# Hybrid decoder block on one core: layer-norm steps with costs of their own, the first head's loads inside the last projection, and a fixed order at the start

## The chip, the cores and the metric

The kernel runs on one core of one Trainium2 chip. The core has five engines that run side by side and are tied together by semaphores: PE (TensorE, matrix products), DVE (VectorE), ACT (ScalarE, function tables), POOL (GpSimd) and SP (SyncE, which here issues the loads and stores). The time is device time in microseconds for one execution; lower is better. The time before is 1504.86 us, the median of two runs (1503.34 and 1506.37).

## The reference, cut to what matters

```python
h = rmsnorm(x, norm_gain)                               # x is 1024 x 1024
proj = h @ w_in                                         # 1024 x 11264
a_val, a_glu, a_gate, q, k, v, r_gate, g_a, g_b = split(proj)
u = a_val * sigmoid(a_glu)
u = depthwise_causal_conv(u, 31 taps) + bias            # each channel alone
u = silu(layernorm(u, ln_g, ln_b))                      # over the 1024 channels
u = u * silu(a_gate)
y_a = u @ w_conv_proj
q, k = rotary(q), rotary(k)                             # 4 heads of 256
o = retention(q, k, v)                                  # causal, chunks of 128 tokens
y_b = (groupnorm(o) * gn_g * silu(r_gate)) @ w_ret_proj
m = sigmoid(g_a) * y_a + sigmoid(g_b) * y_b
out = rmsnorm(x + m @ w_out, final_gain)
```

All of it is float32. Products are formed from a rounded high part and a low remainder of each operand, three matmuls for one.

## The kernel before, in words

**Start.** `row_stats(hf)` squares the half `hf` of x on ACT, adds the squares on DVE (lines 490 to 493), sums them over channels on PE, takes the root on POOL (line 137) and spreads the row factors with a diagonal matrix `dg` (line 503) through PE. `normed` (line 511) multiplies x by them on DVE, `h_split` makes high and low parts. The projections of the first two pairs run beside this.

**Projections.** 88 column blocks of `w_in` are worked off in 44 *pairs* (class `Pair`). A pair forms two blocks for all tokens in seven products (a Strassen scheme) of 12 matmuls of 128x512 each. `prep` builds the seven weight operands on ACT and DVE, in six steps; `use.c` disposes of the results: `Plain` stores them (with Silu for the gates `rg` and `ag`, with Sigmoid for `ga` and `gb`), `Rope` rotates q and k on DVE and POOL and stores them, `Conv` multiplies by the Sigmoid of the gate and queues 31 taps of the convolution. The order is v0, v1, cv0, v2, k0, v3, cv1, q0 and so on (in this document pairs are counted from 0; k pairs are 4, 9, 15 and 20, q pairs 7, 12, 17 and 23, the last conv pair cv7 is 30); the last eight pairs are the gates `ga` and `gb`, all Sigmoid.

**The planner.** The pair loop keeps a budget `left`: after each product it gains `SLOT * FILL` (2.64 us) minus what the product itself costs DVE, then runs at most one `prep` step, and then as many entries of the queue `taps` as the budget holds, each at the price `TAP`. Behind the last conv pair the steps of `layer_norm()` are put behind the taps in the same queue, at the same price each, with empty `idle` steps between. What is left when the pairs are done is emitted behind them.

**Layer norm.** `mean` over `acc`, the sum of the convolution's results; for each of 8 blocks `center`: load `co_d`, subtract `mu` (line 385), store `cd_d`, square on ACT, add; then `var` (16 small matmuls and a root), `rows` (`bcast_rows`: `dg` and two matmuls), and for each block `apply`: load `cd_d` and `ag_d`, multiply by the row factors on DVE (line 411), Silu on ACT (line 412), multiply by `ag` on DVE (line 413), store `u_d` (line 414).

**Heads and output.** Eight half heads follow (class `Head`: `load` of k, q and vT, `keys`, `values`, `main`), with the projections `conv_proj` (which needs all of `u_d` through `load_u`), `ret_proj` and `out_proj` between them. `Weights` loads and splits their weights ahead.

**What sets the order.** Each instruction is written once in the program; a scheduler then places the instructions of each engine, by its own estimate of when they can start, so the order on an engine need not be the order of the code. Each engine works through its own list strictly in order. All loads are issued from SP, in one queue with the stores.

Of the kernel before, what the change touches and what calls it, by code (L numbers as in the profile page):

```python
# [11 lines left out]
ALU = mybir.AluOpType  # L12
# [3 lines left out]
NK = D // P  # L16
# [3 lines left out]
TAPS = 31  # L20
# [9 lines left out]
N_SMALL = 8 * TAPS + 8 * 4 + 16 + H + 4  # L30
W_LIVE = 6
SPLIT_AHEAD = 4
SLOT, TAP, FILL = 2.72, 1.28, 0.97


class Group:
# [7 lines left out]
def hybrid_block_kernel(  # L44
# [70 lines left out]
    def mm(ps, l, r, start, stop, onto=False):  # L115
        nc.tensor.matmul(ps, lhsT=l, rhs=r, start=start, stop=stop, skip_group_check=onto)  # L116
# [22 lines left out]


    taps = deque()

    def flush(n):
        while taps and n > 0:
            taps.popleft()()
            n -= 1

# [165 lines left out]
    class Conv:  # L315
# [8 lines left out]
        def c(self, d, hf, x):  # L324
            cb = self.cb
            if d == 0:
                self.g[hf] = small_t("sg")
                nc.scalar.activation(self.g[hf], x, AF.Sigmoid)
                if hf == 0:
                    self.u = sb.tile([P, 1088], F32, tag="u", bufs=2, name=nm("u"))  # L330
                    nc.gpsimd.memset(self.u[:, :HALO], 0.0)
                return
            u = self.u
            nc.vector.tensor_tensor(u[:, HALO + hf * T:HALO + (hf + 1) * T], x, self.g[hf], ALU.mult)
            if hf == 1:
                return
            box = []

            def first():
                box.append(U("cv"))  # L340
                nc.vector.tensor_scalar(box[0], u[:, 0:S], cw[:, cb, 0:1], cb_[:, cb:cb + 1], ALU.mult, ALU.add)

            def tap(k):
                def go():
                    o = box[0]
                    nc.vector.scalar_tensor_tensor(o, u[:, k:k + S], cw[:, cb, k:k + 1], o, ALU.mult, ALU.add)  # L346
                    if k == TAPS - 1:
                        nc.sync.dma_start(co_d[cb], o)
                        if cb == 0:
                            ln["acc"] = U("acc")  # L350
                            nc.scalar.copy(ln["acc"], o)
                        else:
                            nc.vector.tensor_tensor(ln["acc"], ln["acc"], o, ALU.add)
                        box.clear()
                return go

            taps.append(first)
            taps.extend(tap(k) for k in range(1, TAPS))

    def layer_norm():  # L360

# [52 lines left out]
                nc.sync.dma_start(u_d[cb // 2][cb % 2], d)  # L414
            return go

        def idle():
            pass

        steps += [load(0, co_d), idle, mean, load(1, co_d), idle]  # L420
        for cb in range(NK):
            if cb + 2 < NK:
                steps.append(load(cb + 2, co_d))
            steps.append(center(cb))
        steps += [idle, load(0, cd_d), var, idle, load(1, cd_d), idle, rows, idle]
        for cb in range(NK):
            if cb + 2 < NK:
                steps.append(load(cb + 2, cd_d))
            steps.append(apply(cb))
        return steps  # L430

    def silu(name, n, dst):
# [50 lines left out]
    def row_stats(hf):  # L483
# [16 lines left out]
        r4 = rsqrt(ps[:, :NC], NORM_EPS, NC)  # L500
        dg = small_t("dg", (P, NC, P))
        for c in range(NC):
            nc.vector.tensor_scalar(dg[:, c, :], ident, r4[:, c:c + 1], None, ALU.mult)
        r_row[hf] = bank()
        mm(r_row[hf], ones, dg.rearrange("p c i -> p (c i)"), True, True)

    def normed(hf, js):
        for j in js:
# [23 lines left out]
        next(run0)  # L532
        next(run1)

    row_stats(0)
    prep0[0][0]()
    normed(0, (0, 1))
    h_split("B11", b11)
    row_stats(1)
    prep1[0][0]()  # L540
    normed(0, (2, 3))
    h_split("B21", b21)
    prep0[1][0]()
    prep1[1][0]()
    both()
    normed(1, (0, 1))
    sums(b11, b12, b11)
# [30 lines left out]
        nc.sync.dma_start(cs[i], a["cs"][i])  # L578
    nc.sync.dma_start(dmask, a["dmask"])
    pairs[3].load()  # L580

    left = 0.0
    steps = deque(prep[4:])
    for i in range(2, len(pairs)):
        p = pairs[i]
        nxt = pairs[i + 1] if i + 1 < len(pairs) else None
        for n, cost in enumerate(p.run()):
            if nxt and n == 0:
                nxt.load_xy()
            if n == 3 and i + 2 < len(pairs):  # L590
                pairs[i + 2].load()
            if nxt and n == 2:
                steps.extend(nxt.prep())
            left = min(left + SLOT * FILL - cost, 4.0)
            if steps:
                f, cost = steps.popleft()
                f()
                left -= cost
            while left >= TAP and taps:
                taps.popleft()()  # L600
                left -= TAP
        if isinstance(p.use, Conv) and p.use.cb == NK - 1:
            taps.extend(layer_norm())
        if p is qs[-1]:
            cs = None
    while taps:
        taps.popleft()()


    class Weights:  # L610
        def __init__(self):
# [328 lines left out]
    def free(f):  # L940
        add(lambda w: f(), cost=0)
# [12 lines left out]
        plan[H + 2, c] = ret[1][1][2 * c:2 * c + 2] + conv[1][c:c + 1]  # L954
        plan[H + 3, c] = ret[1][2][2 * c:2 * c + 2] + conv[1][NC + c:NC + c + 1]

    free(heads[0].load)
    free(lambda: halves[0].load_u(None))
    free(heads[0].keys)
    free(lambda: heads[0].values(0))  # L960
    free(lambda: heads[0].values(2))
    late = None
    for i, hd in enumerate(heads):
        nxt = heads[i + 1] if i + 1 < len(heads) else None
# [24 lines left out]
    for n, g in enumerate(groups):  # L989
# [2 lines left out]
            ws.split()  # L992
        while g.cost and ws.n_split < len(ws.seq) and ws.live < g.limit and ws.n_split < need + SPLIT_AHEAD:
            ws.split()
        while g.cost and ws.n_load < len(ws.seq) and ws.n_load < ws.n_split + 2:
            ws.load()
        mine = [ws.ready.popleft() for _ in g.weights]
        g.emit(mine)
# [69 lines left out]
```

## Time and profile before

| what | value |
|---|---|
| median of two runs | 1504.86 us |
| profiled execution, whole time | 1509.48 us |
| its span in the trace | 1507.6 us |
| mean granted clock of PE | 0.977 of full speed |
| PE busy | 1386.6 us, 92% of the span |
| DVE busy | 1158.2 us, 77% |
| ACT busy | 576.7 us, 38% |
| POOL busy | 90.2 us, 6% |
| moved by DMA | 200.80 MB, mean 133 GB/s |

The profiled execution is its span and 1.9 us around it; as a whole it lies 4.6 us above the median of the two timed runs. Busy time is the share of the span in which an engine executes; the profile also cuts the span into 40 slices with the busy tenths of each engine, and there PE shows 9 in nearly all slices, with a dip in the first two and in slices 24 and 25, at about 900 to 945 us.

### The profile page before, as it was taken

What the parts mean: (1) busy time and instruction counts of PE and PEld (TensorE: products, weight loads), DVE (VectorE), ACT (ScalarE), POOL (GpSimd) and SP (SyncE); (2) the same over time, 40 slices, a digit from 0 to 9 for tenths busy, and PEclk for the clock granted to TensorE, in tenths of its full rate; (3) what the DMA queues carried; (4) which work ended last, traced back from release to release, by engine and by line L of the source; (5) the groups of instructions that cost most, each with busy time, mean ns of one, the idle gap of its engine ahead of it and who ended that gap; (6) DMA issues with size and microseconds to landing.
All of it is one profiled execution on the core that took longest, in us unless ns stands there. A gap on an engine that the chain in (4) does not pass through costs nothing.

```text
span 1507.6 us, 16563 instructions
## 1 busy us (share of the span) xinstructions
PE 1386.6 (92%) x6184; PEld 1131.8 (75%) x6184; DVE 1158.2 (77%) x1344; ACT 576.7 (38%) x817; POOL 90.2 (6%) x91
## 2 busy tenths in 40 slices
PE   3899999999999999999999990799999899999998
PEld 2688787887887788888888870687877677777776
DVE  4979989989879979898989465665677757547673
ACT  3453332332233344443443343544544334424321
POOL 1001011011201100000000000000000000000000
PEclk9999999999999999999999995899999999999999
DMA  5143332322323332323333488643443456334331
GB/s 194 58 135 107 107 112 71 112 98 86 125 70 112 106 118 84 126 84 126 112 126 112 164 306 332 241 156 126 140 154 113 130 191 210 121 107 149 123 128 56
DMA packets 95504, 200.80 MB, mean 133 GB/s; under 512 B 8896, under 2 KB 25536, under 8 KB 95424
## 3 DMA queue, kind: packets, MB, share of 16 engines
q1 hardware_dynamic: 94272, 197.65, 38.5%
q10 hardware_dynamic: 1152, 2.10, 0.4%
q8 instruction: 48, 0.79, 0.2%
q14 instruction: 32, 0.26, 0.1%
HBM read 143.09 MB, written 56.62 MB: 132 GB/s over the span
## 4 chain that ended last, share of the span: by engine, by line
PE 66%; DVE 19%; DMA 7%; issue 4%; ACT 3%; POOL 1%; SPq 1%; DVEq 0%; POOLq 0%; ACTq 0%
PE ps L116 64%; DVE cv L346 5%; DVE wl L191 2%; DMA q<-q_d 1%; DMA gb<-gb_d 1%; DVE w L633 1%; DMA d<-co_d 1%; DMA Y<-w_v 1%; DVE G L208 1%; DMA u<-u_d 1%; PE ps L709 1%; DVE h L477 1%; POOL rr L137 1%; DVE ps L254 1%; DVE x L511 1%
## 5 line engine op out<-in xcount | busy, mean ns | idle before, releaser
L116 PE MATMUL ps<-h,wh 128*128 128x512 f32 x2112 | 654.6, 391 | 12.4 <-DVE ps L254 8.6
L116 PEld LDWEIGHTS ps<-h,wh 128*128 128x128 f32 x2112 | 396.1, 188 | 101.9 <-DVE ps L254 11.9
L116 PE MATMUL ps<-h,wl 128*128 128x512 f32 x1056 | 411.4, 390 | 0.3 <-DVE wl L191 0.3
L346 DVE SCALAR_TENSOR_TENSOR cv<-u,small,cv 128x1024 f32<-128x1024 f32 x240 | 311.7, 1299 | 3.5
L116 PEld LDWEIGHTS ps<-h,wl 128*128 128x128 f32 x1056 | 198.4, 188 | 41.9 <-DVE wl L191 0.6
L116 PE MATMUL ps<-oT,w 128*128 128x512 f32 x768 | 192.7, 399 | 6.8 <-DVE yb L838 2.2
L116 PEld LDWEIGHTS ps<-oT,w 128*128 128x128 f32 x768 | 142.4, 189 | 39.2 <-ACT oT L799 3.5
L116 PE MATMUL ps<-h,ws 128*128 128x512 f32 x528 | 127.0, 389 | 2.4 <-DVE x L511 2.4
L116 PEld LDWEIGHTS ps<-h,ws 128*128 128x128 f32 x528 | 99.0, 188 | 23.4 <-DVE x L511 2.9
L116 PE MATMUL ps<-w,m 128*128 128x512 f32 x384 | 94.7, 406 | 8.6 <-ACT w L629 6.3
L116 PEld LDWEIGHTS ps<-w,m 128*128 128x128 f32 x384 | 74.6, 196 | 26.4 <-ACT w L629 7.0
L116 PE MATMUL ps<-u,w 128*128 128x512 f32 x384 | 90.9, 392 | 1.6 <-DVE ga L873 1.1
L116 PEld LDWEIGHTS ps<-u,w 128*128 128x128 f32 x384 | 71.3, 188 | 17.8 <-DVE ga L873 1.9
L190 ACT CAST wh<-G 128x1024 fp32r<-128x1024 f32 (+1 forms) x45 | 46.4, 1034 | 77.3 <-DVE G L208 38.9
L137 POOL TENSOR_TENSOR rr<-rs,neg_half 128x1 f32<-128x1 f32 (+2 forms) x35 | 26.5, 757 | 723.3 <-DVE rs L134 723.3
L208 DVE TENSOR_TENSOR G<-X,N 128x1024 f32<-128x1024 f32 x44 | 55.4, 1259 | 18.0 <-PE ps L116 18.0
L190 ACT CAST wh<-Y 128x1024 fp32r<-128x1024 f32 (+1 forms) x45 | 46.4, 1031 | 58.1 <-DVE Y L217 23.7
L191 DVE TENSOR_TENSOR wl<-Y,wh 128x1024 fp32r<-128x1024 f32 (+1 forms) x45 | 57.6, 1282 | 13.5 <-ACT wh L190 13.3
L285 ACT ACTIVATE o<-ps 128x512 f32<-128x512 f32 x60 | 35.8, 597 | 81.4 <-PE ps L116 75.5
L191 DVE TENSOR_TENSOR wl<-N,wh 128x1024 fp32r<-128x1024 f32 (+1 forms) x45 | 58.2, 1294 | 3.1 <-ACT wh L190 2.0
L191 DVE TENSOR_TENSOR wl<-G,wh 128x1024 fp32r<-128x1024 f32 (+1 forms) x45 | 53.8, 1197 | 6.6 <-PE ps L116 6.0
L200 DVE TENSOR_TENSOR X<-X,Y 128x512 f32<-128x512 f32 x44 | 32.4, 737 | 32.1 <-DMA Y<-w_v 11.2
(122 smaller groups left out, 1562.7 us busy)
## 6 DMA issues: line engine op xcount, KB each, us to landing
raw<-w_ret SPq DMA_DIRECT2D x32, 512.0 KB, 4.7
rg_d<-o SPq DMA_DIRECT2D x32, 256.0 KB, 2.5
raw<-w_conv SPq DMA_DIRECT2D x16, 512.0 KB, 4.4
vT<-v_d SPq DMA_DIRECT2D x16, 512.0 KB, 7.4
rg<-rg_d SPq DMA_DIRECT2D x64, 128.0 KB, 3.0
raw<-w_out SPq DMA_DIRECT2D x16, 512.0 KB, 4.5
v_d<-o SPq DMA_DIRECT2D x24, 256.0 KB, 2.2
x<-xT SPq DMA_DIRECT2D x8, 512.0 KB, 6.4
```

Source lines behind the costliest of these rows:

```text
L116: nc.tensor.matmul(ps, lhsT=l, rhs=r, start=start, stop=stop, skip_group_check=onto)
L137: nc.gpsimd.tensor_tensor(r, s, neg_half[:, :n], ALU.pow)
L190: nc.scalar.copy(hi[:, i], x[:, i])
L191: eng.tensor_tensor(lo[:, i], x[:, i], hi[:, i].bitcast(F32), ALU.subtract)
L200: nc.vector.tensor_tensor(X[:, :T], X[:, T:], Y[:, :T], ALU.add)
L208: nc.vector.tensor_tensor(self.G.rearrange("p (n t) -> p n t", t=T), self.X.rearrange("p (n t) -> p n t", t=T), N[:, :T].unsqueeze(1).broa ...
L254: nc.vector.tensor_tensor(pd, pa, s5, ALU.add)
L285: nc.scalar.activation(o, x, self.func)
L346: nc.vector.scalar_tensor_tensor(o, u[:, k:k + S], cw[:, cb, k:k + 1], o, ALU.mult, ALU.add)
L477: nc.vector.tensor_tensor(lo, x, hi.bitcast(F32), ALU.subtract)
L511: nc.vector.scalar_tensor_tensor(x, x, n_g[:, 2 * j + k:2 * j + k + 1], r_row[hf], ALU.mult, ALU.mult)
L633: nc.vector.scalar_tensor_tensor(lo, t, g, hi.bitcast(F32), ALU.mult, ALU.subtract)
```

## The change

The convolution's taps and the layer-norm steps get a price each in the queue (a load and the mean 0, `center` and `apply` 2.5, `var` 0.2, `rows` 1.8, the last tap of a block `2 * TAP`), and the `idle` steps go; `FILL` goes from 0.97 to 1.04, so a product now gains 2.83 us of budget. With `tc.issue_after(row_stats(0))` the instructions of the block that follows are placed behind the last `dg` of the first half. The pair loop stands behind the classes of the heads, so that the loads of the first head (k, q and the two vT) can be emitted after the fifth product's result of the last pair; `load_u` is emitted behind `keys` and `values`, not between `load` and `keys`. The weights of the later projections are loaded four ahead of their split, not two.

```diff
-SLOT, TAP, FILL = 2.72, 1.28, 0.97
+SLOT, TAP, FILL = 2.72, 1.28, 1.04
...
-            taps.append(first)
-            taps.extend(tap(k) for k in range(1, TAPS))
+            taps.append((first, TAP))
+            taps.extend((tap(k), TAP if k < TAPS - 1 else 2 * TAP) for k in range(1, TAPS))
...
-        def idle():
-            pass
-
-        steps += [load(0, co_d), idle, mean, load(1, co_d), idle]
+        def step(f, cost=0.0):
+            steps.append((f, cost))
+
+        step(load(0, co_d))
+        step(load(1, co_d))
+        step(mean)
         for cb in range(NK):
             if cb + 2 < NK:
-                steps.append(load(cb + 2, co_d))
-            steps.append(center(cb))
-        steps += [idle, load(0, cd_d), var, idle, load(1, cd_d), idle, rows, idle]
+                step(load(cb + 2, co_d))
+            step(center(cb), 2.5)
+        step(load(0, cd_d))
+        step(load(1, cd_d))
+        step(var, 0.2)
+        step(rows, 1.8)
         for cb in range(NK):
             if cb + 2 < NK:
-                steps.append(load(cb + 2, cd_d))
-            steps.append(apply(cb))
+                step(load(cb + 2, cd_d))
+            step(apply(cb), 2.5)
...
-            nc.vector.tensor_scalar(dg[:, c, :], ident, r4[:, c:c + 1], None, ALU.mult)
+            last = nc.vector.tensor_scalar(dg[:, c, :], ident, r4[:, c:c + 1], None, ALU.mult)
         r_row[hf] = bank()
         mm(r_row[hf], ones, dg.rearrange("p c i -> p (c i)"), True, True)
+        return last.ins
...
-    row_stats(0)
-    prep0[0][0]()
-    normed(0, (0, 1))
...
+    with tc.issue_after(row_stats(0)):
+        prep0[0][0]()
+        normed(0, (0, 1))
...
-            while left >= TAP and taps:
-                taps.popleft()()
-                left -= TAP
...
+            while taps and left >= taps[0][1]:
+                f, cost = taps.popleft()
+                f()
+                left -= cost
+            for f in ahead.get((len(pairs) - i, n), []):
+                f()
...
-    free(heads[0].load)
-    free(lambda: halves[0].load_u(None))
-    free(heads[0].keys)
-    free(lambda: heads[0].values(0))
-    free(lambda: heads[0].values(2))
+    ahead = {(1, 4): [heads[0].load]}
...
+    heads[0].keys()
+    while taps:
+        taps.popleft()[0]()
+    heads[0].values(0)
+    heads[0].values(2)
+    halves[0].load_u(None)
...
-        while g.cost and ws.n_load < len(ws.seq) and ws.n_load < ws.n_split + 2:
+        while g.cost and ws.n_load < len(ws.seq) and ws.n_load < ws.n_split + 4:
```

How the instructions stand is shown at four places. The names are the tiles of the program, with a number each; an entry reads result, then operands.

PE at the end of the projections, before. `wh` and `wl` with `h` are the last product of the last pair, `invd, acc` is `var`, `dg, ones` is `rows`, `q, k` are the scores of the first head.

```order
L116 MATMUL ps_964_6321<-h_92_508,wh_966_6336 128x512
L116 MATMUL ps_964_6321<-h_91_507,wl_967_6337 128x512
L116 MATMUL ps_984_6465<-invd_67,acc_950_6231 128x1 x8
L116 MATMUL ps_990_6487<-dg_989_6482,ones_66 128x512
L116 MATMUL ps_992_6495<-dg_991_6490,ones_66 128x512
L116 MATMUL ps_1021_6586<-q_1006_6556,k_1005_6554 128x128 x8
```

The same place in the changed kernel.

```order
L116 MATMUL ps_995_6445<-h_92_508,wh_997_6460 128x512
L116 MATMUL ps_995_6445<-h_91_507,wl_998_6461 128x512
L116 MATMUL ps_1009_6562<-q_1003_6523,k_1002_6521 128x128 x8
L666 MATMUL ps_1012_6576<-ident_64,k_1002_6521 128x128 x4
L666 MATMUL ps_1014_6584<-ident_64,k_1002_6521 128x128 x4
```

The scores now follow the last product directly, and `var` and `rows` have left this place. In the changed kernel `var` stands on PE three pairs earlier, between two products.

```order
L116 MATMUL ps_909_5945<-h_75_416,wh_904_5918 128x512
L116 MATMUL ps_909_5945<-h_74_415,wl_905_5919 128x512
L116 MATMUL ps_931_6061<-invd_67,acc_874_5744 128x1 x8
L116 MATMUL ps_919_6005<-h_82_459,wh_914_5965 128x512
L116 MATMUL ps_919_6005<-h_83_460,wh_914_5965 128x512
```

ACT at the `apply` steps, before: behind the last result of the projections (`o`, line 285), the row factors `mu`, one load of a function table, and then the Silu steps one behind the other.

```order
L285 ACTIVATE o_983_6462<-ps_964_6321 128x512
L130 COPY mu_934_6162<-ps_990_6487 128x512
L130 COPY mu_934_6162<-ps_992_6495 128x512
L412 ACT_TABLE_LOAD
L412 ACTIVATE d_981_6446<-d_981_6446,small_63 128x1024
L412 ACTIVATE d_987_6478<-d_987_6478,small_63 128x1024
L412 ACTIVATE d_993_6498<-d_993_6498,small_63 128x1024
```

ACT at the `apply` steps in the changed kernel (line 407 is the Silu, 280 the Sigmoid of a gate pair, 238, 245 and 255 copies out of and into the banks that PE accumulates in, 185 the high parts of the next weights).

```order
L407 ACT_TABLE_LOAD
L407 ACTIVATE d_926_6037<-d_926_6037,small_63 128x1024
L238 COPY ps_949_6154<-ps_947_6140 128x512
L407 ACTIVATE d_928_6041<-d_928_6041,small_63 128x1024
L245 COPY s5_954_6164<-ps_948_6141 128x512
L407 ACTIVATE d_942_6112<-d_942_6112,small_63 128x1024
L185 CAST wh_952_6160<-Y_913_5962 128x1024
L407 ACTIVATE d_945_6136<-d_945_6136,small_63 128x1024
L280 ACT_TABLE_LOAD
L280 ACTIVATE o_960_6216<-ps_949_6154 128x512
L185 CAST wh_958_6200<-N_923_6026 128x1024
L255 COPY ps_948_6141<-ps_947_6140 128x512
```

The Silu steps now stand among the work of the gate pairs, and the tables of Silu and Sigmoid alternate: 8 loads of a table in this stretch, where there was 1.

SP at the last pair in the changed kernel: `gb_d` are the stores of the last two pairs, `u_d3_124` the last store of `apply`, then the first head's loads, and the loads of `u` behind the last result of the projections.

```order
L409 DMA u_d3_124<-d_980_6323 128x1024
L283 DMA gb_d2_99<-o_993_6440 128x512
L620 DMA k_1002_6521<-k_d0_73 128x2x512
L620 DMA q_1003_6523<-q_d0_69 128x2x512
L620 DMA vT_1004_6525<-v_d0_77 128x2x512
L620 DMA vT_1005_6527<-v_d1_78 128x2x512
...
L283 DMA gb_d3_100<-o_1008_6559 128x512
L620 DMA u_1026_6628<-u_d0_121 128x2x512
```

Before, these loads stood behind all eight `apply` steps, which were themselves behind the last projection.

DVE at the start, before: `sq` are the sums of squares, `X<-X,Y` a step that waits for the weights of pair 0, `wl` low parts of weights, `rs` and `dg` the row factors.

```order
L490 TENSOR_TENSOR sq_22_175<-sq_22_175,sq_21_174 128x1024
L200 TENSOR_TENSOR X_15_163<-X_15_163,Y_16_164 128x512
L490 TENSOR_TENSOR sq_24_177<-sq_24_177,sq_23_176 128x1024
L191 TENSOR_TENSOR wl_30_202<-N_10_152,wh_29_201 128x512
L492 TENSOR_TENSOR sq_24_177<-sq_24_177,sq_22_175 128x1024
L191 TENSOR_TENSOR wl_30_202<-N_10_152,wh_29_201 128x512
L493 TENSOR_TENSOR sq_24_177<-sq_24_177 128x512
L490 TENSOR_TENSOR sq_35_219<-sq_35_219,sq_34_218 128x1024
L134 TENSOR_SCALAR rs_25_190<-ps_20_173 128x4
```

The same place in the changed kernel.

```order
L490 TENSOR_TENSOR sq_22_175<-sq_22_175,sq_21_174 128x1024
L490 TENSOR_TENSOR sq_24_177<-sq_24_177,sq_23_176 128x1024
L492 TENSOR_TENSOR sq_24_177<-sq_24_177,sq_22_175 128x1024
L493 TENSOR_TENSOR sq_24_177<-sq_24_177 128x512
L134 TENSOR_SCALAR rs_25_190<-ps_20_173 128x4
L503 TENSOR_SCALAR dg_27_194<-ident_64,rr_26_192 128x128 x4
L186 TENSOR_TENSOR wl_30_202<-N_10_152,wh_29_201 128x512 x2
L195 TENSOR_TENSOR X_15_163<-X_15_163,Y_16_164 128x512
L195 TENSOR_TENSOR X_18_169<-X_18_169,Y_19_170 128x512
L512 SCALAR_TENSOR_TENSOR x_6_142<-x_6_142,small_63,ps_28_199 128x512 x2
```

The sums of squares and the row factors now stand ahead of the steps on the weights.

## Rows read from the trace of the kernel before

**Rows 1.** The page, part 4: shares of the chain that ended last, by engine.

```profile
PE 66%; DVE 19%; DMA 7%; issue 4%; ACT 3%; POOL 1%; SPq 1%; DVEq 0%; POOLq 0%; ACTq 0%
```

**Rows 2.** Windows: stretch, length, busy us of PE, PEld, DVE, ACT, POOL; clock; DMA share; GB/s.

```profile
575.00:600.00 25.00, 25.00 (x112) 20.72 (x111) 24.79 (x25) 10.34 (x15) 0.00 (x0) 1.00 0.31 106
875.00:900.00 25.00, 23.92 (x106) 19.46 (x105) 18.23 (x17) 14.59 (x19) 0.00 (x0) 1.00 0.90 319
900.00:925.00 25.00, 6.41 (x26) 3.80 (x24) 12.58 (x18) 8.11 (x9) 1.65 (x1) 0.68 0.82 295
925.00:950.00 25.00, 5.68 (x27) 5.71 (x28) 9.20 (x8) 5.55 (x5) 0.00 (x0) 0.50 0.99 373
```

**Rows 3.** Timeline of PE, 900 to 962 us: start, length, operation, [idle before <-releaser].

```profile
901.07 1.84 PE L116 MATMUL ps<-invd,acc 128*128 128x1 f32 x16
905.80 3.51 PE L116 MATMUL ps<-dg,ones 128*128 128x512 f32 x4 [2.90 <-DVE dg L127]
944.32 3.75 PE L116 MATMUL ps<-q,k 128*128 128x128 f32 x16 [35.01 <-DMA q<-q_d]
...
961.35 0.62 PE L116 MATMUL ps<-u,w 128*128 128x512 f32 x2
```

**Rows 4.** Timeline of SP, 938 to 940 us: the last `u_d` store and the head's q.

```profile
938.59 0.33 SPq L414 DMA_DIRECT2D u_d<-d  x1
938.97 0.43 SPq L647 DMA_DIRECT2D q<-q_d  x1
```

**Rows 5.** Timeline of DVE at 910 us: the first `apply` step.

```profile
909.97 1.23 DVE L411 TENSOR_TENSOR d<-d,mu 128x1024 f32<-128x1024 f32 x1 [3.44 <-ACT mu L130]
```

**Rows 6.** Timeline of ACT, 909 to 914 us, and GB/s in 40 slices, 909 to 939 us.

```profile
909.95 1.28 ACT L412 ACT_TABLE_LOAD   x1
911.25 2.37 ACT L412 ACTIVATE d<-d,small 128x1024 f32<-128x1024 f32 x2
...
GB/s 404 229 22 0 0 0 0 235 377 268 218 268 229 218 377 431 421 410 404 432 437 421 415 404 421 437 421 421 399 421 437 432 410 399 421 437 426 393 276 202
```

**Rows 7.** Timeline of the start: four rows of DVE, one of ACT, one of PE.

```profile
16.74 0.69 DVE L200 TENSOR_TENSOR X<-X,Y 128x512 f32<-128x512 f32 x1 [8.82 <-DMA Y<-w_v]
...
28.77 2.72 DVE L511 SCALAR_TENSOR_TENSOR x<-x,small,ps 128x512 f32<-128x512 f32 x4 [1.03 <-PE ps L116]
...
35.39 0.16 DVE L134 TENSOR_SCALAR rs<-ps 128x4 f32<-128x4 f32 x1 [2.76 <-PE ps L116]
...
47.72 2.36 DVE L515 TENSOR_TENSOR x<-x,x 128x1024 f32<-128x1024 f32 x2
...
8.18 1.06 ACT L488 ACTIVATE sq<-x 128x1024 f32<-128x1024 f32 x1 [0.24 <-DMA x<-xT]
...
39.61 1.84 PE L116 MATMUL ps<-h,wh 128*128 128x512 f32 x2
```

**Rows 8.** Timeline of ACT: the copy behind the first product of a pair (pairs 2, 5, 6, 7, 9, 43).

```profile
90.06 0.57 ACT L243 COPY ps<-ps 128x512 f32<-128x512 f32 x1 [1.19 <-PE ps L116]
...
147.17 0.57 ACT L243 COPY ps<-ps 128x512 f32<-128x512 f32 x1 [2.10 <-PE ps L116]
...
167.96 0.57 ACT L243 COPY ps<-ps 128x512 f32<-128x512 f32 x1 [1.61 <-PE ps L116]
...
187.00 0.57 ACT L243 COPY ps<-ps 128x512 f32<-128x512 f32 x1 [2.10 <-PE ps L116]
...
225.08 0.57 ACT L243 COPY ps<-ps 128x512 f32<-128x512 f32 x1 [1.41 <-PE ps L116]
...
883.68 0.59 ACT L243 COPY ps<-ps 128x512 f32<-128x512 f32 x1
```

**Rows 9.** Timeline of DVE and POOL, 245 to 250 us, in pair 9 (k1).

```profile
245.05 2.32 DVE L346 SCALAR_TENSOR_TENSOR cv<-u,small,cv 128x1024 f32<-128x1024 f32 x1
246.24 2.28 POOL L308 TENSOR_TENSOR rs<-rs,ro 128x512 f32<-128x512 f32 x1
249.52 1.27 DVE L346 SCALAR_TENSOR_TENSOR cv<-u,small,cv 128x1024 f32<-128x1024 f32 x1
```

More of the change, by code (lines that the diff above doesn't have):

```diff
@@ L141, in hybrid_block_kernel @@
     taps = deque()
-    def flush(n):
-        while taps and n > 0:
-            taps.popleft()()
-            n -= 1
     zrow = small_t("zrow", (P, T), F32R)
@@ L533, in both @@
         next(run1)
-    row_stats(0)
-    prep0[0][0]()
-    normed(0, (0, 1))
[L538 to L544, printed above, removed]
+    with tc.issue_after(row_stats(0)):
+        prep0[0][0]()
+        normed(0, (0, 1))
+        h_split("B11", b11)
+        row_stats(1)
+        prep1[0][0]()
+        normed(0, (2, 3))
+        h_split("B21", b21)
+        prep0[1][0]()
+        prep1[1][0]()
     both()
@@ L580, in hybrid_block_kernel @@
     pairs[3].load()
[L582 to L598, printed above, removed]
-            while left >= TAP and taps:
-                taps.popleft()()
-                left -= TAP
[L602 to L607, printed above, removed]
     class Weights:
@@ L955, in hybrid_block_kernel @@
         plan[H + 3, c] = ret[1][2][2 * c:2 * c + 2] + conv[1][NC + c:NC + c + 1]
-    free(heads[0].load)
-    free(lambda: halves[0].load_u(None))
-    free(heads[0].keys)
-    free(lambda: heads[0].values(0))
-    free(lambda: heads[0].values(2))
+    ahead = {(1, 4): [heads[0].load]}
+    left = 0.0
+    steps = deque(prep[4:])
+    for i in range(2, len(pairs)):
+        p = pairs[i]
+        nxt = pairs[i + 1] if i + 1 < len(pairs) else None
+        for n, cost in enumerate(p.run()):
+            if nxt and n == 0:
+                nxt.load_xy()
+            if n == 3 and i + 2 < len(pairs):
+                pairs[i + 2].load()
+            if nxt and n == 2:
+                steps.extend(nxt.prep())
+            left = min(left + SLOT * FILL - cost, 4.0)
+            if steps:
+                f, cost = steps.popleft()
+                f()
[3 more added lines that the diff above has]
+                f()
+                left -= cost
+            for f in ahead.get((len(pairs) - i, n), []):
+                f()
+        if isinstance(p.use, Conv) and p.use.cb == NK - 1:
+            taps.extend(layer_norm())
+        if p is qs[-1]:
+            cs = None
+    heads[0].keys()
[4 more added lines that the diff above has]
+    halves[0].load_u(None)
     late = None
```

## The prediction, made before the result was known

> **What bounds the kernel now.** I read the shares of the last chain first. PE carries 66% of it, DVE 19%, DMA 7% [rows 1], so the kernel is a PE program with places at which PE waits for something else, and each place has to be looked at alone. The windows show three kinds. In the middle of the projections (575 to 600 us) PE is busy 25.00 of 25.00 us and DVE 24.79 [rows 2]: PE is the bound, with DVE close behind. At 875 to 900 us, where the centre steps of the layer norm run beside the last pairs, PE still has 23.92 of 25 [rows 2]. From 900 to 950 us PE has 6.41 and 5.68 us of 50 while DMA is busy 0.82 and 0.99 [rows 2], and the clock granted to PE falls to 0.50, the lower of its two levels. That is the hole of this kernel. PE's timeline says what is in it: `var` at 901.07, `rows` at 905.80, then 35.01 us of waiting until the q of the first head has landed, scores at 944.32, and steady work again with the first product of u at 961.35 [rows 3]. The wait is named after q, but q's load was issued at 938.97, right behind the last `u_d` store at 938.59 [rows 4]: what PE waits for are the eight `apply` steps, which take from 909.97 to 938.59 at 28.6/8 = 3.58 us each [rows 4, 5], and in that stretch DMA runs at some 421 GB/s [rows 6].
>
> The projections themselves have a fixed pace. Pairs 7 and 8 take 225.08 - 187.00 = 38.08 us, 19.04 each [rows 8]. From pair 2 (90.06) to pair 43 (883.68) there are 41 pairs, 793.62 us, where 41 x 19.04 = 780.64: 13.0 us are stalls. Pair 5, behind k0, takes 167.96 - 147.17 = 20.79, 1.75 too long [rows 8]; taken so from the same view, some 7.9 us come with the four k pairs, 2.4 with the four q pairs, 0.75 elsewhere in the middle and 1.9 in pairs 42 and 43. The reason is seen in pair 9: a tap that takes 1.27 us alone takes 2.32 beside POOL's addition of 2.28 [rows 9], so in a Rope pair DVE, already full, falls behind.
>
> **The change, part by part.** The sum is made against the profiled execution of 1509.48 us, and its difference is then taken off the median of 1504.86.
>
> *A. The hole.* The order shows PE going from the last product straight to the scores, with `var` three pairs earlier, and SP issuing the head's loads about a pair before they are needed. If that holds, the wait of 35.01 us for q and of 2.90 for `dg` are gone: -37.9. The matmuls of `var` (1.84) and `rows` (3.51) [rows 3] only move; they still run, so I count nothing for them. What is late next is the chain from the scores to the first product of u: 944.32 to 961.35, 17.0 us [rows 3], in which DVE masks the scores, splits keys, queries and values and then splits u. That chain is in the changed kernel too, and as u is now loaded behind the last store of the last pair, its transfer, issued about 1 us after the last product, has these 17 us to land in; I count nothing. Nothing else covers it: if u lands later than the splits ahead of it are done, each us shows. Less would be gained if the head starts later than the last product (bound -33, some 5 us), more if the clock does not fall in a hole that is now about 20 us, since the scores' 3.75 us and some 3 more were run at 0.50 (bound -41). I take -38, the two waits.
>
> *B. The start.* Before, DVE waits 8.82 us for the Y of pair 0, until 16.74, with the second sum of squares queued behind it [rows 7]. Its operand was ready at 8.18 + 1.06 = 9.24. In the new order the sums follow at once: 9.24 plus three additions (1.2, 1.2, 0.7) is about 12.1, two us for the small matmuls, two for POOL, 0.9 for `dg` gives 17.1, then two low parts and two X steps (1.4 each two), the second X bound by its load at about 19; `normed` starts at about 19.9, where it was 28.77. Not all of this reaches PE: the second half's sums still need their small matmuls on PE, and its row factors stand ahead of the first product (39.61) on PE. They end at about 31 (before: the factors could start at 35.39 [rows 7]), so the first product stands at about 35.7, 3.9 earlier; the later products wait for the difference at 47.72, which comes at about 41.6 by the same count of DVE steps, 6.1 earlier. I take -5, between them; the bounds are -3 (DMA, which runs at its full rate at the start, sets the pace of pairs 0 to 2 instead) and -6.5.
>
> *C. More taps in the Rope pairs.* The larger budget puts 6, 5, 5, 5 taps into the four q pairs by the order, where there were 3, 0, 0, 0; the k pairs keep 5. The k pairs cost 7.9/4 = 2.0 us each, the q pairs 2.4/4 = 0.6. If q pairs become like k pairs, that is 4 x 1.4 = 5.5 us; a little comes back since pair 42 loses its centre steps. I take +5, with 0 (the slack is enough) and +9 (four times 2.3) as bounds. The taps end three or four pairs earlier, which is what makes room for D.
>
> *D. The layer norm beside the projections.* `mean` and the centre steps move to pairs 38 to 40, all `apply` steps to pairs 40 to 42. DVE has room there, as no taps are left: 8 x (1.23 + 1.24) = 20 us over three pairs of 57. ACT has less: in the two pairs that hold most of them 8 Silu of 1.19 (2.37 for two), 8 table loads of 1.30 (909.95 to 911.25 [rows 6]) and 7.9 us a pair of copies, casts and the like (10.34 in 25 us [rows 2]), so 9.5 + 10.4 + 15.8 = 36 us of 38.1. DMA has none to spare either: 8 x 3 tiles of 0.52 MB are 12.6 MB, the two pairs' own traffic 2 x 2.1, together 16.8 MB, at 421 GB/s 39.9 us in 38.1. Both just fit, so the cover is thin: a copy that PE waits for now stands behind a Silu whose own input hangs on DVE and a load. The nearest row is the second window, where the centre steps took 319 GB/s and DMA was 0.90 busy and PE lost 1.1 us in 25. For three pairs that is 57/25 x 1.1 = 2.5: I take +3. The bounds are 0 and +13 (all eight loads of a table on PE's path, 10.4, and the 3).
>
> *E. Without price.* The head's loads in the last pair are 2.1 MB, 5 us of DMA beside 19 us; the raw weights four ahead change the order of DVE, PE and ACT behind the first head nowhere that I could see, and what hides them before (seven buffers filled well ahead) hides them now.
>
> Sum: -38 - 5 + 5 + 3 = -35. The profiled execution would be about 1474.5, the median 1504.86 - 35 = 1470.
>
> **The rivals.** *First, ACT and DMA become the bound of pairs 40 to 42.* For it: 36 of 38.1 us on ACT, in an order fixed beforehand, and 39.9 of 38.1 on DMA. Against it: PE had 23.92 of 25 with DMA at 0.90. If each table load costs twice what the row shows, because ACT stands empty before it while its next operand waits, ACT needs 36 + 10.4 = 46.5 in 38.1 us, 8.4 more: 1478 to 1480, the middle of the loss being 10. [...]
>
> *Second, the change doesn't do what it says*: the last `apply` steps slip past the last product, because the loads of `cd_d` and `ag_d` stand in SP's queue behind stores that wait for ACT. For it: the order counts places and not times. If four steps slip, 4 x 3.58 us follow the last product, and then about 9 us for the stores and the loads of u: 23 us of the gain, 1493.
>
> *Third, slower than before.* Each of the eight `apply` steps holds PE up, since ACT's list is in order: a Silu waits for DVE, DVE for the load, and PE's copy for the Silu. Its price is the steps' own pace of 3.58 plus two switches of 1.30, 6.2 each, 49 in all: -35 - 3 + 49 = +11, 1516. It decides from (35 + 3)/8 = 4.8 us for each step. Against it: in pairs 42 and 43 the squares of the centre steps stand on ACT in the same way, and cost 1.9 us in two pairs.
>
> **How the numbers follow.** The forecast, 1470 with 1462 to 1477 as its own range, gets 0.64. The first rival (1477 to 1485) gets 0.20, the second 0.06, the third 0.03, and a better outcome (below 1462, where the clock stays up, C costs nothing and B is full) 0.07. The bounds of the terms, added as independent, reach from -42 to -23, that is 1463 to 1482; with the rivals the range is 1459 to 1486, which leaves out the second and the third rival, the tail of the first and half of the better outcome. Two per cent, about what a measurement of this kernel can tell from no change, lie at 1474.8, close to the forecast: faster by more than 2% gets 0.68 (the better outcome and most of the forecast), within 2% 0.30, slower by over 2% (above 1535, beyond even the third rival) 0.02.
>
> **What would show it.** A: PE's timeline has the scores within 2 us of the last product, with no wait for q, and the first product of u some 17 us later; a wait for u there, or `apply` behind the last product, shows the second rival. B: `normed` at about 20 us, the first product at about 36, the first product of pair 2 some 5 us earlier than 90.06. C: pairs 7, 12, 17 and 23 and those behind them longer than 19.04. D: pairs 40 to 42 longer by 3 us in all; if by 10, waits of PE for ACT's copies (lines 238, 245, 255) behind Silu or table loads show the first rival, by 50 the third. The prediction is wrong above all if pairs 40 to 42 don't keep their pace, since the thin cover of D is the only place where a few us decide.

## The result and the profile after

The changed kernel takes 1471.53 us (median of two runs, 1469.30 and 1473.75) where 1504.86 were measured before: the ratio is 0.9761, with a 95% interval of 0.973 to 0.9792. That is 33.3 us less; 35 were forecast, and 1459 to 1486 was the range. The profiled execution took 1469.30 us with a span of 1467.5, at a granted clock of 0.990; its span is 40.1 us shorter than the one profiled before, since the two profiled executions lie at opposite ends of their kernels' runs.

The windows of the changed kernel, with the columns of [rows 2], show what became of the hole.

```profile
575.00:600.00 25.00, 25.00 (x112) 20.71 (x111) 24.69 (x27) 10.87 (x16) 0.00 (x0) 1.00 0.31 95
855.00:880.00 25.00, 23.56 (x104) 18.97 (x103) 19.06 (x20) 21.02 (x24) 0.00 (x0) 1.00 0.89 298
...
905.00:930.00 25.00, 17.98 (x91) 13.71 (x91) 15.80 (x21) 16.58 (x23) 0.55 (x1) 0.92 0.66 213
930.00:955.00 25.00, 25.00 (x117) 20.99 (x117) 15.97 (x22) 8.07 (x13) 0.56 (x1) 0.94 0.83 292
```

Where PE had 12 us of work in 50 [rows 2] there is now one window in which it lacks 7 us, and the granted clock in these two windows is 0.92 and 0.94. The stretch of the `apply` steps is the second row: ACT is 21.02 us busy of 25, DMA 0.89, and PE still has 23.56.

PE's timeline of the changed kernel answers to [rows 3].

```profile
843.30 1.84 PE L116 MATMUL ps<-invd,acc 128*128 128x1 f32 x16
850.13 1.88 PE L116 MATMUL ps<-dg,ones 128*128 128x512 f32 x4
...
911.40 1.95 PE L116 MATMUL ps<-q,k 128*128 128x128 f32 x16
...
925.55 0.73 PE L116 MATMUL ps<-u,w 128*128 128x512 f32 x2 [1.75 <-ACT w L602]
926.50 0.80 PE L116 MATMUL ps<-u,w 128*128 128x512 f32 x1 [0.22 <-ACT w L602]
928.75 12.46 PE L116 MATMUL ps<-u,w 128*128 128x512 f32 x45 [1.45 <-DVE w L603]
```

`var` and `rows` run among the projections, at full clock (a granted 1.00; `rows` takes 1.88 us, before 3.51 at 0.56), the scores follow the last product at once with no wait for q, and they too take 1.95 us, not 3.75. The first product of u comes 14.2 us later, steady work 17.35 us later, after waits for the split of its weights. That the scores are shorter brought nothing: from them to the scores of the second head it takes 37.2 us before and 37.8 after.

The start, DVE's rows and then one of PE, answers to [rows 7].

```profile
9.32 1.23 DVE L490 TENSOR_TENSOR sq<-sq,sq 128x1024 f32<-128x1024 f32 x1 [1.36 <-ACT sq L488]
...
19.96 2.72 DVE L512 SCALAR_TENSOR_TENSOR x<-x,small,ps 128x512 f32<-128x512 f32 x4
...
41.05 2.35 DVE L516 TENSOR_TENSOR x<-x,x 128x1024 f32<-128x1024 f32 x2
...
34.20 1.84 PE L116 MATMUL ps<-h,wh 128*128 128x512 f32 x2
```

The copies behind the first product of pairs 2, 5, 6, 7, 9 and 38 answer to [rows 8].

```profile
86.12 0.57 ACT L238 COPY ps<-ps 128x512 f32<-128x512 f32 x1 [1.19 <-PE ps L116]
...
143.24 0.57 ACT L238 COPY ps<-ps 128x512 f32<-128x512 f32 x1 [5.61 <-PE ps L116]
...
164.05 0.57 ACT L238 COPY ps<-ps 128x512 f32<-128x512 f32 x1 [1.57 <-PE ps L116]
...
183.09 0.57 ACT L238 COPY ps<-ps 128x512 f32<-128x512 f32 x1 [1.89 <-PE ps L116]
...
223.03 0.57 ACT L238 COPY ps<-ps 128x512 f32<-128x512 f32 x1 [1.41 <-PE ps L116]
...
792.71 0.57 ACT L238 COPY ps<-ps 128x512 f32<-128x512 f32 x1 [2.12 <-PE ps L116]
```

Cut at the same points of the program, the two spans compare so (the last product ends where PE goes on to its next work, 901.07 and 911.40; pair 38 starts at 786.57 before, by the same view as [rows 8]):

| stretch | before | after | difference | forecast |
|---|---|---|---|---|
| start to pair 2 | 90.06 | 86.12 | -3.9 | B, -5 |
| pair 2 to pair 38 | 696.5 | 706.6 | +10.1 | C, +5 |
| pair 38 to the last product's end | 114.5 | 118.7 | +4.2 | D, +3 |
| to the scores of the second head (981.56, 949.21) | 80.5 | 37.8 | -42.7 | A, -38 |
| to the end | 526.0 | 518.3 | -7.7 | 0 |

The last line is not the change's: the stretch from the second head's scores to the end, whose order the change leaves alone but for the raw weights, takes 517.7 to 526.0 us in the fourteen profiles of this study, 521.9 in a second profile of the changed kernel itself and 517.7 in one with the raw weights two ahead. It holds most of the 6.8 us by which the profiled executions differ more than the medians.

### The profile page after: what moved, and what is told of

It is laid out like the page before. It is cut to its first block, busy times and chain, and to the rows that moved or that the text cites. A ratio compares the mean times of both kernels' runs of the same rounds, so it can differ in the third digit from the quotient of the medians.

```text
span 1467.5 us, 16559 instructions
## 1 busy us (share of the span) xinstructions
PE 1387.2 (95%) x6184; PEld 1129.2 (77%) x6184; DVE 1156.1 (79%) x1344; ACT 584.2 (40%) x824; POOL 86.5 (6%) x91
## 5 line engine op out<-in xcount | busy, mean ns | idle before, releaser
L116 PEld LDWEIGHTS ps<-h,wl 128*128 128x128 f32 x1056 | 199.4, 189 | 42.7 <-DVE wl L186 0.6
L116 PEld LDWEIGHTS ps<-oT,w 128*128 128x128 f32 x768 | 143.4, 191 | 37.8 <-ACT oT L772 3.2
L811 DVE TENSOR_TENSOR yb<-ps,yb 128x512 f32<-128x512 f32 x48 | 32.9, 687 | 31.0 <-PE ps L116 30.9
```

What stands on the lines that cost most here:

```text
L811: nc.vector.tensor_tensor(y, ps, y, ALU.add)
```

## The experiments

All times are medians; before ran 1504 to 1508 on the same chips.

**Which line makes the room.** The kernel before with one number changed:

```diff
-SLOT, TAP, FILL = 2.72, 1.28, 0.97
+SLOT, TAP, FILL = 2.72, 1.28, 1.04
```

> The kernel before with one number changed, FILL 1.04 for 0.97; old prices, idle steps, start and raw weights as before. My theory: the larger budget alone ends the taps early enough for the whole layer norm to stand ahead of the last product, so the hole closes to about 14 to 17 us and only the start's 4 us are missing: about 1475 (1471 to 1480). Rival: the steps' own prices and the missing idle steps make the room; then the hole of 60 us stays and the dearer Rope pairs come on top: 1505 to 1515.

It took 1472.23 us, ratio 0.9781 (0.976 to 0.9803): within the spread of these runs as fast as the whole change. Pairs 2 to 38 take 706.4 us, the price of C is there in full. One pair goes worse than in the change, pair 39, where `var` stands: PE's timeline, and in a second fence DVE's.

```profile
827.52 1.19 PE L116 MATMUL ps<-h,wh 128*128 128x512 f32 x2 [3.41 <-DVE ps L254]
828.65 3.57 PE L116 MATMUL ps<-invd,acc 128*128 128x1 f32 x16
```

```profile
821.09 1.23 DVE L385 TENSOR_TENSOR d<-d,mu 128x1024 f32<-128x1024 f32 x1 [3.23 <-DMA d<-co_d]
...
826.77 0.69 DVE L254 TENSOR_TENSOR ps<-ps,s 128x512 f32<-128x512 f32 x1
```

DVE waits 3.23 us for the load of a centre step, a sum of that pair (line 254) stands behind it, and PE waits 3.41 us for the sum. The granted clock is 0.63 from 825 to 835 us (`var` takes 3.57 us, not 1.84), and the pair is 9.8 us too long, 845.52 - 816.65 = 28.87. That the old prices set the centre steps too close here is likely, but was not tried by itself. The layer norm also ends earlier, u is loaded among the last stores, and from the last product (923.54) to the second head's scores (953.01) there are 29.5 us, not 37.8. That is 8.3 us less, where the stretch from pair 38 to the scores is 8.1 longer (126.8 us for 118.7): the two cancel.

The opposite, the whole change with the old number:

```diff
-SLOT, TAP, FILL = 2.72, 1.28, 1.04
+SLOT, TAP, FILL = 2.72, 1.28, 0.97
```

> The changed kernel with FILL back at 0.97; everything else of the change stays. My theory: the Rope pairs lose their extra 10 us, but the eight apply steps stand behind the last product again, at 3.6 us each, with their stores and the loads of u behind them: 1471.5 - 10 - 3.5 + 32 = about 1490 (1483 to 1497). Rival (the prices do it, the larger budget only costs): about 1460.

1509.49 us, ratio 1.0032 (1.0016 to 1.0047): a little slower than before. I had only the `apply` steps fall behind the last product; PE's timeline shows that nearly all of the layer norm does.

```profile
902.79 3.43 PE L116 MATMUL ps<-q,k 128*128 128x128 f32 x16 [2.92 <-DMA q<-q_d]
915.80 3.57 PE L116 MATMUL ps<-invd,acc 128*128 128x1 f32 x16 [8.71 <-DVE acc L388]
922.36 3.75 PE L116 MATMUL ps<-dg,ones 128*128 128x512 f32 x4 [2.98 <-DVE dg L127]
...
966.62 13.10 PE L116 MATMUL ps<-u,w 128*128 128x512 f32 x48 [7.98 <-ACT w L602]
```

The head's scores now come early, but `var` and `rows` follow them and u is 64 us behind the scores. The stalls are smaller, but by 6 us and not by the 10 I had expected (pairs 2 to 27 take 491.0 us, 497.1 in the changed kernel). So the prices and the missing idle steps gain nothing by themselves.

**The start alone**, left out of the change:

```diff
-    with tc.issue_after(row_stats(0)):
+    row_stats(0)
+    if True:
```

> The changed kernel without the fixed order at the start. My theory: pair 2 starts 3.9 us later and nothing gives it back: 1475.4 (1474 to 1477). Rival: the loads or DVE set the pace of the first pairs and the saturated Rope pairs swallow the lead: 1471.5, no change.

1477.20 us, ratio 0.9817 (0.9781 to 0.9854); the interval overlaps that of the changed kernel, so the time alone does not decide. In its profile pair 2 starts at 92.00. With the fixed order it started at 85.5 to 88.1 in eleven profiles, without it at 90.06, 90.33 and 92.00. In four of these fourteen profiles PE was granted less than the full clock on the way (a mean of 0.94 or 0.95 in a window between 30 and 92 us): in this one, and in the three with the fixed order that start pair 2 at 88.0 or 88.1; the other eight start it at 85.5 to 86.2. Like compared with like, the gain is 3.9 to 4.9 us at full clock and 3.9 to 4.0 with the dip. Later pairs don't swallow it; pairs 2 to 38 take 706.2 us here.

**The head's loads.** They go out early without the line `ahead` as well. The kernel with the budget alone emits them behind the pair loop, and still SP's timeline has the load of q some 25 us ahead of the scores (923.54).

```profile
898.94 0.37 SPq L647 DMA_DIRECT2D q<-q_d  x1
```

So the scheduler puts the loads there by itself once `apply` is out of the way. To see what they are worth they had to be held back by force, behind the last store (`st`, kept by `Plain`):

```diff
-            nc.sync.dma_start(self.dst[d][:, hf * T:(hf + 1) * T], o)
+            hop['st'] = nc.sync.dma_start(self.dst[d][:, hf * T:(hf + 1) * T], o)
...
-    ahead = {(1, 4): [heads[0].load]}
+    ahead = {}
...
+    with tc.issue_after(hop['st'].ins):
+        heads[0].load()
     heads[0].keys()
```

> The changed kernel with the first head's loads forced behind the last store of the last pair. My theory: PE waits for q, issued about 1.5 us behind the last product and 5 us under way, before the chain to the first product of u can begin, and u's loads stand behind 2.1 MB more: 6 to 8 us, 1478 to 1480. Rival: DVE's chain of splits is the bound in that gap and has work of its own meanwhile: under 2 us, 1472 to 1473.

1483.17 us, ratio 0.9859 (0.983 to 0.9887), 10 to 12 us over the changed kernel, more than I gave. A row of SP's timeline and one of PE's:

```profile
914.95 0.49 SPq L620 DMA_DIRECT2D q<-q_d  x1
...
921.12 3.58 PE L116 MATMUL ps<-q,k 128*128 128x128 f32 x16 [7.68 <-DMA q<-q_d]
```

The wait for q is 7.68 us, and the scores take 3.58 us, where they take 1.95 in the changed kernel and took 3.75 before, at a granted clock of 0.50.

**The changed kernel again, and the order of u.**

> The changed kernel as it is, on the chip of the next three: 1471 (1469 to 1475), for their comparison.

1473.62 us, ratio 0.9787 (0.9756 to 0.9819). Beside it, `load_u` where it was before the change:

```diff
-    heads[0].keys()
     while taps:
         taps.popleft()[0]()
+    halves[0].load_u(None)
+    heads[0].keys()
     heads[0].values(0)
     heads[0].values(2)
-    halves[0].load_u(None)
```

> The changed kernel with load_u emitted ahead of keys and values, as before the change. My theory: the loads of u then stand among the last pair's stores, u is split while the scores run, and the gap from the last product to the first product of u shrinks from 14.0 us to some 9 to 10, as in the run with the larger budget alone (9.1): 1467 (1465 to 1469). Rival: the splits of u stand ahead of the head's own on DVE, so the head starts later by as much: 1471.

1472.87 us, ratio 0.9787 (0.9758 to 0.9817): no difference, and from the scores (910.32) to the second head's (949.78) 39.5 us, where the changed kernel beside it has 37.9. So the time is the rival's. Its reason, that splits of u ahead of the head's own only change places with them, fits this, but was not tried by itself.

**The table loads.** Sigmoid for Silu in the `apply` steps leaves out the multiplication by the normalised value and all eight switches:

```diff
-                nc.scalar.activation(d, d, AF.Silu, bias=ln_b[:, cb:cb + 1], scale=ln_g[:, cb:cb + 1])
+                nc.scalar.activation(d, d, AF.Sigmoid, bias=ln_b[:, cb:cb + 1], scale=ln_g[:, cb:cb + 1])
```

> The changed kernel with Sigmoid in place of Silu in the eight apply steps (the layer norm's result is not multiplied by itself then), so that ACT stays in one table from the gates on and seven of the eight table loads fall away. My theory: ACT had room for them, and PE waited only 1.4 us in those pairs: 1470 to 1471. The first rival of the prediction (table loads and Silu stand in the way of the copies PE waits for): 8 x 1.3 us less, 1461 to 1463.

1474.06 us, ratio 0.9795 (0.9766 to 0.9824): nothing gained in the time. ACT's timeline shows an `apply` step with no load ahead of it; in the changed kernel, second fence, there is one.

```profile
854.97 2.38 ACT L407 ACTIVATE d<-d,small 128x1024 f32<-128x1024 f32 x2 [0.79 <-DVE d L406]
857.26 0.58 ACT L238 COPY ps<-ps 128x512 f32<-128x512 f32 x1
```

```profile
853.16 1.28 ACT L407 ACT_TABLE_LOAD   x1
854.45 1.25 ACT L407 ACTIVATE d<-d,small 128x1024 f32<-128x1024 f32 x1
855.60 0.58 ACT L238 COPY ps<-ps 128x512 f32<-128x512 f32 x1
```

From pair 38 to the scores this kernel takes 910.51 - 793.82 = 116.7 us, 2.0 less than the changed one. The changed kernel itself takes 118.7 and 118.6 us there in its two profiles. So eight switches cost PE 2 us and not 8 to 10; ACT had the room.

**The stalls of the Rope pairs.** First without POOL's subtraction and addition (the rotation is left incomplete):

```diff
-                nc.gpsimd.tensor_tensor(ac, ac, bs, ALU.subtract)
-                nc.gpsimd.tensor_tensor(bc, bc, as_, ALU.add)
```

> The changed kernel without POOL's subtractions and additions in the Rope pairs (q and k are stored without the second product of the rotation). My theory: the stalls of some 21 us behind the Rope pairs come from POOL slowing DVE's taps; without it DVE has the 8 x 2.5 us more and they fall below 8: about 1457 (1453 to 1461). Rival: the taps and DVE's own four products a pair fill DVE in any case: the stalls stay, 1468 to 1471.

1451.97 us, ratio 0.9648 (0.9622 to 0.9675): 21.7 us less than the changed kernel beside it, the stalls are gone altogether. Then with the same sums on DVE, which gives the reference's result:

```diff
-                nc.gpsimd.tensor_tensor(ac, ac, bs, ALU.subtract)
-                nc.gpsimd.tensor_tensor(bc, bc, as_, ALU.add)
+                nc.vector.tensor_tensor(ac, ac, bs, ALU.subtract)
+                nc.vector.tensor_tensor(bc, bc, as_, ALU.add)
```

> The changed kernel with the rotation's subtraction and addition on DVE in place of POOL; the result is the reference's. My theory: what stalls PE behind the Rope pairs is that a DVE tap beside POOL takes 2.3 us for 1.3, four to five us a pair, while the four sums take DVE itself 4 x 0.69 = 2.8 us: most of the 21 us of stalls goes, 1473 - 16 = 1457 (1453 to 1463). Rival: without POOL's sums the stalls went because the tiles of the rotation came free earlier or because less was to be done; DVE then has 22 us more work in pairs in which it is full: 1473 to 1485.

1451.55 us, ratio 0.9643 (0.9626 to 0.9661): again all of it, more than I had dared to say. Pair 4 (k0) on POOL and DVE in the changed kernel:

```profile
140.15 1.67 POOL L304 TENSOR_TENSOR rs<-rs,ro 128x512 f32<-128x512 f32 x1 [108.00 <-DVE rs L298]
...
143.03 2.27 POOL L304 TENSOR_TENSOR rs<-rs,ro 128x512 f32<-128x512 f32 x1
...
140.59 0.68 DVE L298 TENSOR_TENSOR rs<-ps,cs 128x512 f32<-128x512 f32 x1
141.85 0.69 DVE L299 TENSOR_TENSOR ro<-ps,cs 128x512 f32<-128x512 f32 x1 [0.58 <-POOL rs L304]
142.46 1.69 DVE L341 SCALAR_TENSOR_TENSOR cv<-u,small,cv 128x1024 f32<-128x1024 f32 x1
144.07 2.31 DVE L186 TENSOR_TENSOR wl<-N,wh 128x1024 fp32r<-128x1024 f32 x1
```

And with the sums on DVE, DVE's timeline, and in a second fence the copies on ACT behind the first products of pairs 5 and 6:

```profile
140.58 0.69 DVE L304 TENSOR_TENSOR rs<-rs,ro 128x512 f32<-128x512 f32 x1
141.19 0.69 DVE L303 TENSOR_TENSOR rs<-rs,ro 128x512 f32<-128x512 f32 x1
...
144.19 1.29 DVE L341 SCALAR_TENSOR_TENSOR cv<-u,small,cv 128x1024 f32<-128x1024 f32 x1
145.38 1.22 DVE L186 TENSOR_TENSOR wl<-N,wh 128x1024 fp32r<-128x1024 f32 x1
```

```profile
143.21 0.57 ACT L238 COPY ps<-ps 128x512 f32<-128x512 f32 x1 [5.59 <-PE ps L116]
...
162.25 0.57 ACT L238 COPY ps<-ps 128x512 f32<-128x512 f32 x1 [2.13 <-PE ps L116]
```

Pair 5 now takes 162.25 - 143.21 = 19.04 us, as do all from 2 to 37 within 0.04. Beside POOL the low part of the weights takes 2.31 us for 1.22, a tap 1.69 for 1.29 (up to 2.32 in other pairs), while the product of a PSUM tile with a table takes its 0.68 us beside POOL too.

The next kernel adds to this that two weights are split in the last pair (for that the code that plans the heads, not shown here, is moved ahead of the pair loop):

```diff
-    ahead = {(1, 4): [heads[0].load]}
+    ahead = {(1, 4): [heads[0].load], (1, 6): [ws.split] * 2}
```

> The same, and the first two weights of the projection after u split into their parts during the last pair, not behind the splits of u. My theory: of the gap of 14 us between the last product and steady work on u some 3.5 us are waits for these splits on ACT and DVE: 3 us below the kernel with the rotation on DVE alone. Rival: the splits of u end last in any case: no difference of over 1 us.

1451.04 us, ratio 0.9647 (0.9629 to 0.9665). From the scores to those of the second head it takes 927.86 - 892.99 = 34.9 us, 37.4 without the early split: 2.5 us in the profile, 0.5 in the time, which the runs can't tell from nothing.

**A budget by stretch**, on the changed kernel:

```diff
-            left = min(left + SLOT * FILL - cost, 4.0)
+            left = min(left + SLOT * (0.97 if i < 25 else 1.08) - cost, 4.0)
```

> The changed kernel with FILL 0.97 up to pair 24 and 1.08 from pair 25 on. My theory: the Rope pairs take fewer taps and stall 6 to 10 us less, and the plain pairs take the rest, with the last apply step some 10 us ahead of the last product: 1466 (1462 to 1470). Rival: DVE, 97 to 99% busy in the plain pairs already, can't take more, and the stalls or the apply steps slip to the end: 1472 to 1485.

1477.50 us, ratio 0.9823 (0.9807 to 0.9839); it fell to the rival. Pairs 2 to 27 give 7.5 us back, as expected, but the layer norm ends too late, and PE's timeline has the gap again:

```profile
912.17 3.75 PE L116 MATMUL ps<-q,k 128*128 128x128 f32 x16 [4.54 <-DMA q<-q_d]
...
934.24 6.14 PE L116 MATMUL ps<-u,w 128*128 128x512 f32 x16 [7.86 <-ACT w L602]
```

**The version that is best here** puts together the sums on DVE, a larger budget, u ahead of the head's keys, and the early split (the plan of the heads is moved as above):

```diff
-SLOT, TAP, FILL = 2.72, 1.28, 1.04
+SLOT, TAP, FILL = 2.72, 1.28, 1.07
...
-                nc.gpsimd.tensor_tensor(ac, ac, bs, ALU.subtract)
-                nc.gpsimd.tensor_tensor(bc, bc, as_, ALU.add)
+                nc.vector.tensor_tensor(ac, ac, bs, ALU.subtract)
+                nc.vector.tensor_tensor(bc, bc, as_, ALU.add)
...
-    ahead = {(1, 4): [heads[0].load]}
+    ahead = {(1, 4): [heads[0].load], (1, 6): [ws.split] * 2}
...
-    heads[0].keys()
     while taps:
         taps.popleft()[0]()
+    halves[0].load_u(None)
+    heads[0].keys()
     heads[0].values(0)
     heads[0].values(2)
-    halves[0].load_u(None)
```

> The rotation's sums on DVE, FILL 1.07, the loads of u emitted ahead of keys and values, and the first two weights split in the last pair: all of u is then split by the end of the last product. My theory: with the stalls of the Rope pairs gone DVE has the room for a larger budget, the last apply step ends a pair earlier, and the gap from the last product to steady work on u shrinks from 17 us to about 9: 1451.5 - 6 = 1445 (1441 to 1448). Rival: the larger budget brings the stalls back, as it did in the change: 1452 to 1460.

1443.11 us, ratio 0.958 (0.9555 to 0.9604), where before took 1508.23 beside it. PE's timeline:

```profile
893.15 1.95 PE L116 MATMUL ps<-q,k 128*128 128x128 f32 x16
...
896.59 3.21 PE L116 MATMUL ps<-u,w 128*128 128x512 f32 x13
...
903.76 6.96 PE L116 MATMUL ps<-u,w 128*128 128x512 f32 x30
```

The first product of u comes 3.4 us behind the scores and fills the pauses of the head, and steady work on u begins 10.6 us behind them. No pair from 2 to 35 is longer than 19.05 us: the larger budget does not bring the stalls of the Rope pairs back. Pairs 36 to 40, where the layer norm now stands, are 10.7 us longer together, its own work on PE included (8.6 in pairs 38 to 42 with the sums on DVE alone). From the scores to the second head's (919.89) there are 26.7 us, 37.4 with the sums on DVE alone. Of the three further edits the early split gave 0.5 us alone, and u ahead of the keys nothing at the old budget; the larger budget was not tried by itself, nor how they work together.

## Why the prediction was right, point by point

**A, the hole: right in cause, some 5 us short.** PE no longer waits for q or `dg` (the -37.9), and steady work on u starts 17.35 us behind the last product, as 17.0 had been carried over. What I left out is that `var` and `rows`, 1.84 and 3.51 us, also leave this stretch: 37.9 + 5.4 = 43.3 of the measured 42.7. I had said that they only move, which is true; but then they had to stand in D. The bound of -41, for a clock that stays up, rested on shorter scores; they are shorter, and as said this brought nothing.

**B, the start: right in size, not in the path.** `normed` begins at 19.96 (19.9 forecast), the difference at 41.05 (41.6), the first product at 34.20 (35.7), and pair 2 starts 3.9 us earlier. But the first product itself is 5.4 us earlier and the difference 6.7, more than the 3.9 and 6.1 of the forecast. What decided is a later wait of PE for `normed`, before and after:

```profile
57.38 3.01 PE L116 MATMUL ps<-h,ws 128*128 128x512 f32 x12 [2.45 <-DVE x L511]
...
53.43 3.02 PE L116 MATMUL ps<-h,ws 128*128 128x512 f32 x12 [2.64 <-DVE x L512]
```

It ends 3.95 us earlier, and that lead lasts up to pair 2. DMA did not set the pace: between 30 and 60 us it is busy 0.08.

**C, the taps: the term that was mis-sized.** It cost 10.1 us where I took +5 with +9 as the bound. The q pairs did what was forecast: their stalls went from 2.4 to 7.8 us, +5.4 for 5.5. But the k pairs, counted as unchanged, went from 7.9 to 13.4. Two sums over the traces say what it was not. It was not taps of their own: a k pair and the one behind it, all four together, hold 54 taps before and 53 after (a q pair and the one behind it 20 and 45). And POOL does not slow DVE much more than it did: what DVE's operations beside POOL's sums take beyond the median of their kind comes to 21.7 us before and 23.7 after, while the stalls up to pair 38 go from 11.1 to 21.2. What has shrunk is DVE's idle time, from 39.1 to 31.7 us in pairs 4 to 24. So the forecast failed in pricing each pair by its own taps; that DVE lacks the slack to make good for the same slowing fits these sums, but no run changes the slack by itself. With `FILL` alone changed the same 10 us lie elsewhere, 12.5 us of stalls on the q pairs and 6.5 on the k pairs. That the stalls as a whole come from POOL's sums is shown: both kernels without them have none. In the rows of pair 4 above, an operation of DVE with two inputs in SBUF takes 2.31 us beside POOL's sums for 1.22 without them, and one with an input in PSUM takes its 0.68 us beside them too; what makes this difference was not tried by itself.

**D, the layer norm beside the projections: the size right, the reason not.** 4.2 us were lost for 3 forecast, but 3.7 of them are the matmuls of `var` and `rows` (1.84 and 1.88). The thin cover of ACT and DMA held: PE waited 1.44 us in these pairs, once, where it had waited 1.08 before. One reading of before was wrong: the 1.9 us put down to the squares in pairs 42 and 43 lie in pairs 41 and 42, and nearly all of it is the work of `mean` on PE.

```profile
859.81 1.88 PE L116 MATMUL ps<-acc,invd 128*128 128x512 f32 x4
```

So that row was no evidence against the third rival; the 1.44 us of waits after the change are. The first rival is refuted by the kernel without switches, which gains 2.0 us in the stretch and nothing in the time; each of the eight table loads takes ACT 1.28 us, as in [rows 6], with at most 0.05 us of idle time ahead of it and 0.09 behind. That a load costs twice its row, the condition of that rival, was an estimate that no run shows.

**E: right as far as the profiles can tell.** With the raw weights two ahead (the kernel with the budget alone) the rest of the program takes 517.7 us, 518.3 and 521.9 with four ahead.

**The sum.** -3.9 + 10.1 + 4.2 - 42.7 = -32.3, beside -35 forecast and -33.3 by the medians: C was 5 too small and A 5 too small, and they cancelled. That the sum came so close is in part luck. **What I had wrong about the change itself** lies outside the sum: I gave the closing of the hole to prices, early loads and order together. The runs show that the one number `FILL` does it, that the prices alone do nothing, that the head's loads go out early without `ahead`, and that the second rival (steps that slip past the end) is what happens at 0.97, and in a milder form with the budget by stretch.

## What to carry to other kernels

When a list of steps spills over the end of a long stage, look first at what sets the pace of the queue ahead of it: here one number, and not the steps' own prices, decided whether 60 us were exposed. Price every operation that moves in the stretch where it lands as well as in the one that it leaves; two terms of this sum were wrong by 5 us each, A for want of that, and C since a pair was priced by its own taps alone. And before giving a full vector engine less work, look at whether its instructions run at their own length: taking 32 small sums away from the engine beside it and giving them to the full one gained 22 us.

## What the runs showed of the hardware that was not expected

Moving POOL's 32 sums to DVE lowered DVE's busy time only from 1156.1 to 1152.0 us, though PE's stalls of 21 us went to none; without the sums altogether DVE is busy for 1135.0. So POOL's sums cost DVE 21 us, and doing them itself costs 17, nearly as much; that the 17 cost PE nothing and the 21 cost it 21 is not a matter of the amount; before the change about the same slowing stalled PE for 10.3 us behind the Rope pairs. A likely reason, argued and not shown, is that the scheduler sees the sums when they are DVE's own and lays the taps around them, but does not see that POOL slows DVE, so that the instructions that take 2.31 us for 1.22 fall just where PE waits for the next operand. The part of DVE's waits for tiles that POOL still held (2.9 us in five waits) is small beside it.
